# Layer 0's channel mixer by seven products of quarters, context tokens plain or as a fifth pair, and the step between the layers rebuilt

## The chip, the cores and the metric

The kernel runs on one core of one Trainium2 chip. The metric is device time in microseconds of that core for one launch, as the median of several runs. TensorE multiplies, VectorE, ScalarE and GpSimd (PE, DVE, ACT, POOL in the rows) work on tiles in SBUF, and the loads and stores spoken of here are issued from SyncE (SP).

## The reference, cut to what matters

Two layers work on 1024 latent tokens and 256 context tokens of width 1024. Each has a token mixer and then a channel mixer with 2816 hidden features; modulation vectors (six a layer, from `silu(c) @ ada_w + ada_b`) shift, scale and gate both. In the last layer the context is dropped.

```python
def _conv_ffn(h, w_gate, w_up, conv_w, conv_b, w_down):
    a = h @ w_gate
    ap = jnp.pad(a, ((0, 0), (1, 1), (0, 0)))
    a = ap[:, :-2] * conv_w[0] + ap[:, 1:-1] * conv_w[1] + ap[:, 2:] * conv_w[2] + conv_b
    return (jax.nn.silu(a) * (h @ w_up)) @ w_down
...
        x = x + g1 * _rmsnorm(y_l, norm_g[layer, 1])
        f_l = _conv_ffn(_modulate(_rmsnorm(x, norm_g[layer, 2]), sh2, sc2), ffn_w_gate[layer],
                        ffn_w_up[layer], ffn_conv_w[layer], ffn_conv_b[layer], ffn_w_down[layer])
        x = x + g2 * _rmsnorm(f_l, norm_g[layer, 3])
```

Layer 0 does the same for the context tokens (`xc`), with weights shared and a convolution of their own.

## The kernel before

**Arithmetic.** Every float32 operand is split in a high part (a cast) and a low part (the rest after it); `mm3` multiplies hi·hi, hi·lo and lo·hi, so each product of 128 contracted rows is three matmuls, up to 512 columns wide. ScalarE makes most of the high parts, GpSimd or VectorE the low ones.

**Layer 0's channel mixer (`ffn`)** walks over 22 tiles j of 128 features. For each: gate for the two latent blocks of 512 tokens (`pg`), gate and up for the 256 context tokens (`pc`), up for the latents (`pu`), each 8 contraction tiles; the convolution, Silu and product on ScalarE and VectorE; and down for the tile j-1 before, in 20 units (10 token tiles by two halves of 512 columns), each one `mm3` into a `dn` bank which VectorE adds into ten accumulators in SBUF (L909). The units are put between the groups of gate and up, as are single steps of the modulation's matmuls for later vectors (`ada_steps`, up to three a tile).

**`between_layers`** finishes the units of the last tile, does residual and norm for each token tile, transposes pairs of tiles to feature order (`to_feature`), and multiplies each block of 256 tokens by 512 columns of layer 1's input weights (480 matmuls of 256 columns, stored as `hv`); then the modulation vectors (1, 2) and (1, 3). `odd_in`, layer 1's input projection, follows.

**Layer 1's channel mixer (`ffn_seven`)** already runs by seven products: features, tokens and contraction are cut in two, four quarter blocks of each operand are combined by sums and differences, and seven products of half size replace eight (P1 to P7; `B11`, `B21`, `B22`, `T1` to `T4` on the token side, `A11`, `A12`, `A22`, `S1` to `S4` on the weight side). A pair of feature tiles is two halves (gate, up) of 7 x 12 matmuls. The hidden values' combinations go to DRAM (`gs`) and come back for the down stage (`ffn_down`, `down_operands`), again seven products, here over four pairs of token tiles; `left` loads `sr` and casts it to `sh`, `sl`, `right` does the down weights' sums.

**What sets the order.** The program is written engine-neutrally and a scheduler orders each engine's instructions; each engine then runs them strictly in that order, and a tile's next use waits until its buffers are free (`raw` has 3, `whi` and `wlo` 4 each). `ada_unit` makes one modulation vector: 8 loads of 512 KB and 32 matmuls, with the bias added as a matmul against a row of ones (L305) from `brow`; the sum is copied to `mrow`, of which there is one buffer.

Of the kernel before, what the change touches and what calls it, by code (L numbers as in the profile page):

```python
# [10 lines left out]
F32 = mybir.dt.float32  # L11
# [11 lines left out]
OUT_SLOTS = ((4, 3, 1), (3, 4, 1))  # L23
# [5 lines left out]
P = 128  # L29
# [29 lines left out]
class Kernel:  # L59
# [55 lines left out]
    def run(self):  # L115
        nc, tc = self.nc, self.tc
        with ExitStack() as es:
# [13 lines left out]
            with ExitStack() as eh:  # L131
                h = self.htiles(eh.enter_context(self.hpool()))
                self.out_proj(0, h)
                self.ffn(0, h)
                with ExitStack() as em:
                    self.odd_in(h, eh, em)
                    self.mla(em)
            with ExitStack() as es:
                self.ffn_operands(es)
                self.out_proj(1, None)  # L140
                self.ffn_seven(1, es)
# [34 lines left out]
    def differences(self, cs, names):  # L176

        F = self.F
        for n in names:
            out, x, y = {"T1": ("T1", "B12", "B11"), "T2": ("B11", "B22", "T1"), "T3": ("B12", "B22", "B12"),  # L180
                         "T4": ("B21", "B11", "B21")}[n]
            self.nc.vector.tensor_tensor(out=F[out][:, :, cs], in0=F[x][:, :, cs], in1=F[y][:, :, cs], op=ALU.subtract)

# [114 lines left out]
    def ada_unit(self, ps, tag, l, v, wp, bufs):  # L298
# [3 lines left out]
        brow = wp.tile([1, D], F32, tag="raw", name="brow", bufs=bufs)  # L302
        nc.sync.dma_start(brow, I["ada_b"][l:l + 1, v * D:(v + 1) * D])
        for g in range(4):
            nc.tensor.matmul(acc[32 * g:32 * g + 32, :256], self.ones[0:1, 0:32], brow[:, 256 * g:256 * g + 256],  # L305
                             start=True, stop=False)
        for k in range(KD):
            raw = wp.tile([P, D], F32, tag="raw", name="raw", bufs=bufs)
            nc.sync.dma_start(raw, I["ada_w"][l, k * P:(k + 1) * P, v * D:(v + 1) * D])
            for g in range(4):  # L310
                nc.tensor.matmul(acc[32 * g:32 * g + 32, :256], self.sT[:, k, :], raw[:, 256 * g:256 * g + 256],
                                 start=False, stop=k == KD - 1)
            yield
        row = self.cp.tile([P, 256], F32, tag="mrow", name="mrow", bufs=1)
        nc.vector.tensor_copy(row, acc[:, :256])
# [45 lines left out]
    def to_feature(self, ps, pool, xns, h, b0, l, which, width=512, bufs=2, every=2):  # L361
# [5 lines left out]
        for k in range(KD):  # L367
# [7 lines left out]
            eng = nc.gpsimd if k % every == 0 else nc.vector  # L375
# [6 lines left out]
    def gate_row(self, pool, l, gi, r):  # L382

        nc, I = self.nc, self.I
        ngb = pool.tile([P, D], F32, tag="xin", name="ngb", bufs=3)
        g = I["norm_g"]
        nc.sync.dma_start(ngb, bass.AP(g.tensor, (l * 4 + 1 + 2 * gi) * D, [[0, P], [1, D]]))
        gb = pool.tile([P, D], F32, name="gb", tag="gb", bufs=1)
# [4 lines left out]
    def residual(self, pool, y, gb, xsrc, xdst, pw=False):  # L393
        nc = self.nc
        x = pool.tile([P, D], F32, tag="xin", name="xin", bufs=3)
        nc.sync.dma_start(x, xsrc)
        t = pool.tile([P, D], F32, tag="yt", name="yt", bufs=2)
# [399 lines left out]
    def out_proj(self, l, h):  # L797
        nc, tc, I = self.nc, self.tc, self.I
        nt = 10 if l == 0 else 8
        with ExitStack() as es:  # L800
# [29 lines left out]
            tts = list(range(nt)) if l == 0 else [0, 1, 4, 5, 2, 3, 6, 7]  # L830
            for tt in tts:
# [9 lines left out]
                last = l == 1 and tt == tts[-1]  # L841
                if last:
                    self.wgs = self.seven_weights(self.gate_raws(0))
                    next(self.wgs)
                    wg = next(self.wgs)
                with tc.manual_schedule(engines={mybir.EngineType.PE, mybir.EngineType.DVE}) if last else ExitStack():
# [8 lines left out]
                    xns.append(self.residual(tp, y, gb, xs, xd, True))  # L855
                    if last:
                        self.first = [self.plain_products(wg, self.pse)]
                    self.flush(pst, tp, xns, h, tt, l, 3)

    def gate_raws(self, p, which="ffn_w_gate"):  # L860
        w = self.I[which][1][:, 256 * p:256 * p + 256].rearrange("(k p) c -> p k c", p=P)
        return [self.raw_w(w[:, 4 * i:4 * i + 4, :], 4, 256) for i in range(2)]

    def flush(self, ps, tp, xns, h, tt, l, which):
        if len(xns) == 2 and l == 1:
            self.to_quarters(ps, xns, (tt - 1) * P, l)
            if tt == 5:
                self.differences(slice(0, 256), ("T1", "T2", "T3", "T4"))
            xns.clear()
        elif len(xns) == 2:  # L870
            self.to_feature(ps, tp, xns, h, (tt - 1) * P, l, which, 256)
            xns.clear()


    def ffn(self, l, h):
        nc, tc, I = self.nc, self.tc, self.I
        nt = 10 if l == 0 else 8
        ctxb = l == 0
        cw = self.cw[l]
        wide = T if ctxb else NL  # L880
        with ExitStack() as eo:
            ap = eo.enter_context(tc.tile_pool(name="facc", bufs=1, reuse_waits="tile"))
            acc = [ap.tile([P, D], F32, name=f"acc{i}") for i in range(nt)]
            tp = eo.enter_context(tc.tile_pool(name="ff", bufs=2, reuse_waits="tile"))
            with ExitStack() as es:
                pgp = es.enter_context(tc.tile_pool(name="psG", bufs=1, space=PSUM, reuse_waits="tile"))
                psd = eo.enter_context(tc.tile_pool(name="psD", bufs=3, space=PSUM, side="right", reuse_waits="tile"))
                ps = es.enter_context(tc.tile_pool(name="psF", bufs=1, space=PSUM, side="right", reuse_waits="tile"))
                self.nw, self.wx = 0, tp

                def weights(j):
                    c = slice(j * P, (j + 1) * P)
                    g = self.split_w(I["ffn_w_gate"][l][:, c].rearrange("(k p) c -> p k c", p=P), KD, P)
                    u = self.split_w(I["ffn_w_up"][l][:, c].rearrange("(k p) c -> p k c", p=P), KD, P)
                    return g, u

                def down_w(j):
                    return self.split_w(I["ffn_w_down"][l, j * P:(j + 1) * P, :][:, None, :], 1, D)

                def down_units(j, g, w):  # L900
                    def unit(tt, hf):
                        o = slice(hf * 512, hf * 512 + 512)
                        c = slice(tt * P, (tt + 1) * P)
                        pd = psd.tile([P, 512], F32, tag="dn", name="dn")
                        self.mm3(pd, g[0][:, c], g[1][:, c], w[0][:, 0, o], w[1][:, 0, o], True, True)
                        if j == 0:
                            nc.scalar.copy(acc[tt][:, o], pd)
                        else:
                            nc.vector.tensor_tensor(out=acc[tt][:, o], in0=pd, in1=acc[tt][:, o], op=ALU.add)  # L909
                    return [(lambda tt=tt, hf=hf: unit(tt, hf)) for tt in range(nt) for hf in range(2)]  # L910

                def group(dst, w, b0, bn):
                    for k in range(KD):
                        self.mm3(dst, w[0][:, k, :], w[1][:, k, :], h[0][:, k, b0:b0 + bn], h[1][:, k, b0:b0 + bn],
                                 k == 0, k == KD - 1)

                def conv(j, a, src):
                    n = src.shape[1]
                    nc.scalar.activation(a, src, AF.Identity, bias=cw[:, 66 + j:67 + j], scale=cw[:, 22 + j:23 + j])
                    nc.vector.scalar_tensor_tensor(out=a[:, 1:], in0=src[:, :n - 1], scalar=cw[:, j:j + 1],  # L920
                                                   in1=a[:, 1:], op0=ALU.mult, op1=ALU.add)
                    nc.vector.scalar_tensor_tensor(out=a[:, :n - 1], in0=src[:, 1:], scalar=cw[:, 44 + j:45 + j],
                                                   in1=a[:, :n - 1], op0=ALU.mult, op1=ALU.add)
                    nc.scalar.activation(a, a, AF.Silu)

                def finish(a, src, gh, gl, eng=nc.gpsimd):
                    nc.vector.tensor_tensor(out=a, in0=src, in1=a, op=ALU.mult)
                    nc.scalar.copy(gh, a)  # L928
                    eng.tensor_tensor(out=gl, in0=a, in1=gh.bitcast(F32), op=ALU.subtract)  # L929

                steps = self.ada_steps(psd, "dn", [(0, 5), (1, 0), (1, 1)] if l == 0 else [])
                pend = []
                wgu = weights(0)
                for j in range(NF):
                    nu = len(pend)
                    done = [0]

                    def some(frac):
                        while done[0] < min(nu, math.ceil(nu * frac)):
                            pend[done[0]]()  # L940
                            done[0] += 1
                        if frac != 0.4 and frac != 0.8:
                            next(steps, None)

                    wg, wu = wgu
                    a = tp.tile([P, wide], F32, tag="a", name="a", bufs=2)
                    gh = tp.tile([P, wide], F32R, tag="gh", name="gh", bufs=2)
                    gl = tp.tile([P, wide], F32R, tag="gl", name="gl", bufs=2)
                    pg = pgp.tile([P, NL], F32, tag="pg", name="pg", bufs=1)
# [902 lines left out]
```

## Time and profile before

| | before |
|---|---|
| median of 3 runs | 3232.47 us (3231.61 to 3233.96) |
| profiled execution, its own time | 3232.91 us |
| its span | 3231.10 us |
| mean granted clock of TensorE | 0.984 |
| TensorE, VectorE, ScalarE, GpSimd busy | 95%, 54%, 36%, 28% |
| layer 0's first gate matmul; last up matmul's end | 674.29; 1599.18 us |
| end of layer 0's down; start of layer 1's projection | about 1623; 1722.33 us |
| layer 1's gate and up; its down | 2562.01 to 3001.04; to 3222 us |

The shares are means over stages with different limits, so the stretch of the change is read by its own windows and by start times on the timeline. A matmul's duration is a latency: consecutive ones overlap, and the distance between their starts is what each costs. PEclk is the granted share of the full clock of 2.4 GHz; 0.5 is the lower level, 1.2 GHz.

### The profile page before, as it was taken

The numbers are of one execution on the slowest core, as the hardware profiler recorded it, in microseconds if no ns is written. First come the engines' busy times: TensorE is split into PE (matmuls) and PEld (weight loads), VectorE is DVE, ScalarE is ACT, GpSimd is POOL, SyncE is SP. The second block draws the span as 40 slices with busy tenths as digits, with TensorE's granted clock in tenths as the row PEclk, the third lists the DMA queues.
The fourth block names the chain that finished last, engine by engine and source line by source line (L and its number), as shares of the span: only waits on it lengthen the run. The fifth ranks groups of instructions, "written<-read, shape, count | busy, mean of one in ns | idle before, by whom it ended". The sixth has DMA issues, their size and how long they took to land. (4 is left out here: it accounts for less than half of the span.)

```text
span 3231.1 us, 42059 instructions
## 1 busy us (share of the span) xinstructions
PE 3081.5 (95%) x16660; PEld 2546.0 (79%) x16660; DVE 1733.4 (54%) x2476; ACT 1175.9 (36%) x1925; POOL 905.7 (28%) x652
## 2 busy tenths in 40 slices
PE   7998899999999999999999999998999999999998
PEld 4876788777778888888777878786797788888787
DVE  5254776532434444444563434444555597788674
ACT  4212776442111111111262233333675433333343
POOL 2122223132222222222232223333321245555001
PEclk8999999999999999999999999999999999999999
DMA  7555333331221111111162451004534233333784
GB/s 235 173 172 173 83 86 120 118 118 60 66 85 60 39 40 40 40 40 40 61 227 93 137 184 31 24 29 144 175 89 138 92 96 107 98 98 107 256 287 147
DMA packets 285363, 355.72 MB, mean 110 GB/s; under 512 B 18349, under 2 KB 215522, under 8 KB 285166
## 3 DMA queue, kind: packets, MB, share of 16 engines
q1 hardware_dynamic: 253086, 310.26, 30.6%
q10 hardware_dynamic: 32080, 42.78, 3.8%
q8 instruction: 131, 2.15, 0.3%
q14 instruction: 66, 0.54, 0.0%
HBM read 271.28 MB, written 81.69 MB: 109 GB/s over the span
## 5 line engine op out<-in xcount | busy, mean ns | idle before, releaser
L909 DVE TENSOR_TENSOR acc<-dn,acc 128x512 f32<-128x512 f32 x420 | 279.7, 686 | 330.7 <-PE dn L102 330.4
L91 POOL TENSOR_TENSOR wlo<-raw,whi 128x1024 fp32r<-128x1024 f32 x94 | 225.6, 2404 | 657.8 <-ACT whi L90 627.3
L100 PE MATMUL acc<-hhi,whi 128*128 128x512 f32 (+3 forms) x632 | 236.1, 374 | 0.0
L102 PE MATMUL acc<-hhi,wlo 128*128 128x512 f32 (+3 forms) x632 | 229.9, 364 | 1.2 <-POOL wlo L91 1.2
L101 PE MATMUL acc<-hlo,whi 128*128 128x512 f32 (+3 forms) x632 | 229.5, 363 | 0.0
L90 ACT CAST whi<-raw 128x1024 fp32r<-128x1024 f32 x94 | 98.2, 1045 | 310.0 <-PE pu L101 167.0
L353 POOL TENSOR_TENSOR ss<-ss,mhalf 128x1 f32<-128x1 f32 (+1 forms) x122 | 72.0, 591 | 453.0 <-DVE ss L352 453.0
L100 PE MATMUL dn<-whi,gh 128*128 128x512 f32 x360 | 143.5, 399 | 4.3 <-DVE acc L909 4.3
L100 PE MATMUL acc<-whi,hhi 128*128 128x256 f32 (+1 forms) x464 | 143.5, 315 | 3.3 <-DVE hhi L374 3.0
L188 POOL TENSOR_TENSOR wlo<-raw,whi 128x512 fp32r<-128x512 f32 (+1 forms) x66 | 114.8, 1752 | 110.2 <-ACT whi L187 110.2
L102 PE MATMUL acc<-whi,hlo 128*128 128x256 f32 (+1 forms) x464 | 139.7, 311 | 3.8 <-POOL hlo L376 3.1
L102 PE MATMUL dn<-whi,gl 128*128 128x512 f32 x360 | 140.6, 391 | 1.2 <-POOL gl L929 1.2
L101 PE MATMUL acc<-wlo,hhi 128*128 128x256 f32 (+1 forms) x464 | 140.0, 305 | 0.8 <-POOL wlo L91 0.8
L101 PE MATMUL dn<-wlo,gh 128*128 128x512 f32 x360 | 140.6, 391 | 0.0
L100 PEld LDWEIGHTS acc<-hhi,whi 128*128 128x128 f32 (+1 forms) x632 | 118.3, 187 | 21.1 <-issue 2.1
L102 PEld LDWEIGHTS acc<-hhi,wlo 128*128 128x128 f32 (+1 forms) x632 | 118.1, 187 | 20.9 <-POOL wlo L91 1.7
L101 PEld LDWEIGHTS acc<-hlo,whi 128*128 128x128 f32 (+1 forms) x632 | 118.3, 187 | 18.3 <-issue 1.2
L188 POOL TENSOR_TENSOR wlo<-st,whi 128x1024 fp32r<-128x1024 f32 x40 | 97.3, 2435 | 101.0 <-ACT whi L187 94.4
L929 POOL TENSOR_TENSOR gl<-a,gh 128x256 fp32r<-128x256 f32 (+1 forms) x44 | 69.1, 1571 | 171.7 <-ACT gh L928 156.7
L100 PE MATMUL pg<-hhi,whi 128*128 128x512 f32 x288 | 114.1, 396 | 0.0
L101 PE MATMUL pg<-hlo,whi 128*128 128x512 f32 x288 | 112.5, 391 | 0.0
L102 PE MATMUL pg<-hhi,wlo 128*128 128x512 f32 x288 | 112.2, 390 | 0.0
(590 smaller groups left out, 8887.2 us busy)
## 6 DMA issues: line engine op xcount, KB each, us to landing
raw<-in_ada_w SPq DMA_DIRECT2D x96, 512.0 KB
raw<-in_ffn_w_down SPq DMA_DIRECT2D x69, 512.0 KB
raw<-in_ffn_w_gate SPq DMA_DIRECT2D x44, 512.0 KB
raw<-in_ffn_w_up SPq DMA_DIRECT2D x44, 512.0 KB
sr<-gs SPq DMA_DIRECT2D x12, 1408.0 KB
raw<-in_od_w_in SPq DMA_DIRECT2D x26, 512.0 KB
gs<-sx SPq DMA_DIRECT2D x11, 1024.0 KB
mx<-mix SPq DMA_DIRECT2D x18, 512.0 KB
```

The costliest lines, as they stand in the source:

```text
L90: nc.scalar.copy(hi, raw)
L91: nc.gpsimd.tensor_tensor(out=lo, in0=raw, in1=hi.bitcast(F32), op=ALU.subtract)
L100: nc.tensor.matmul(out, lh, rh, start=first, stop=False)
L101: nc.tensor.matmul(out, lh, rl, start=False, stop=False)
L102: nc.tensor.matmul(out, ll, rh, start=False, stop=last)
L188: eng.tensor_tensor(out=v(t[1]), in0=x, in1=v(t[0]).bitcast(F32), op=ALU.subtract)
L353: nc.gpsimd.tensor_tensor(out=ss, in0=ss, in1=self.mhalf[:, :ss.shape[1]], op=ALU.pow)
L909: nc.vector.tensor_tensor(out=acc[tt][:, o], in0=pd, in1=acc[tt][:, o], op=ALU.add)
L929: eng.tensor_tensor(out=gl, in0=a, in1=gh.bitcast(F32), op=ALU.subtract)
```

## The change

Layer 0's channel mixer also runs by seven products. `layer0_ffn` replaces `ffn`, with quarters of the latents (11 pairs of feature tiles, 2 halves each, 84 matmuls of 512 columns a half). The 256 context tokens are multiplied plainly within each half ("X", 48 matmuls of 256 columns, between P2 and P6). In down the two context tiles are a fifth pair beside the latents' four; the hidden values go through DRAM (`gs0`). Weights of the next half are prepared while a half runs; the low parts of the four plain weight quarters are VectorE's, those of the sums GpSimd's. Differences of the token quarters are made in place as the output projection finishes its pairs, whose order for layer 0 is now that of layer 1. The first pair's gate runs product by product as its operands come. Modulation steps go one to a half, behind P1.

`layer0_last` does residual and norm, for the tiles 4 to 7 and 9 and then 0 to 3 and 8, as the last product finishes them. The step between the layers takes blocks of two tiles in the order 512, 768, 0, 256, 1024, with three modulation steps each; the low parts there are all VectorE's. `ada_unit` adds the bias on VectorE from four broadcast loads into `mrow`.

```diff
@@ ada_unit @@
-        brow = wp.tile([1, D], F32, tag="raw", name="brow", bufs=bufs)
-        nc.sync.dma_start(brow, I["ada_b"][l:l + 1, v * D:(v + 1) * D])
+        row = self.cp.tile([P, 256], F32, tag="mrow", name="mrow", bufs=1)
         for g in range(4):
-            nc.tensor.matmul(acc[32 * g:32 * g + 32, :256], self.ones[0:1, 0:32], brow[:, 256 * g:256 * g + 256],
-                             start=True, stop=False)
+            nc.sync.dma_start(row[32 * g:32 * g + 32, :],
+                              bass.AP(I["ada_b"].tensor, (l * 6 + v) * D + 256 * g, [[0, 32], [1, 256]]))
...
-        nc.vector.tensor_copy(row, acc[:, :256])
+        nc.vector.tensor_tensor(out=row, in0=acc[:, :256], in1=row, op=ALU.add)
@@ out_proj @@
-            tts = list(range(nt)) if l == 0 else [0, 1, 4, 5, 2, 3, 6, 7]
+            tts = [0, 1, 4, 5, 2, 3, 6, 7, 8, 9][:nt]
...
+                        if l == 0 and tt > 3:
+                            self.differences_in_place(cs)
@@ layer0_ffn @@
+                    def weights(which, p, r=None):
...
+                        put([(A11, first), (A12, second)], ("A11", "A12"), nc.vector)
+                        put([(A21, first), (A22, second)], ("A21", "A22"), nc.vector)
+                        for o, x, y, op in ((self.s1, A21, A22, ALU.add), (A21, A11, A21, ALU.subtract),
+                                            (A11, self.s1, A11, ALU.subtract), (A12, A12, A11, ALU.subtract)):
+                            nc.vector.tensor_tensor(out=o, in0=x, in1=y, op=op)
+                        put([(r0, lambda t: t)], ("S2", "S3"), nc.gpsimd)
+                        put([(self.s1, first), (A12, second)], ("S1", "S4"), nc.gpsimd)
...
+                    alone("P1", "pp", "A11", "B11")
+                    alone("P2", "pp", "A12", "B21")
+                    part("T2", F["B11"], every)
+                    alone("P6", "pp", "S2", "T2")
+                    part("T3", F["B12"], every)
+                    alone("P7", "pp", "S3", "T3")
+                    for k, t in enumerate(t1):
+                        nc.vector.tensor_tensor(out=t, in0=F["B22"][:, k, :], in1=F["B11"][:, k, :], op=ALU.subtract)
+                        part("T1", t, k)
+                    alone("P5", "ada", "S1", "T1")
+                    part("B22", F["B22"], every)
+                    alone("P3", "Y", "S4", "B22")
...
+                    context()
+                    alone("P4", "X", "A22", "T4")
+                    x = context_products(wg)
...
+                        for n, a, b in (("P1", "A11", "B11"), ("P2", "A12", "B21"), ("X", 0, 0), ("P6", "S2", "T2"),
+                                        ("P7", "S3", "T3"), ("P5", "S1", "T1"), ("P3", "S4", "B22"), ("P4", "A22", "T4")):
...
+                for b0 in (512, 768, 0, 256, 1024):
+                    self.to_feature([psx], tb, C[tt:tt + 2], h, b0, 1, 0, 256, 2, None)
+                    for _ in range(3):
+                        next(steps, None)
...
@@ ffn_down @@
-        nq = 4
+        nq = len(accs)
+        t1s, t2s = ([0, 1, 2, 3], [4, 5, 6, 7]) if l else ([0, 1, 2, 3, 8], [4, 5, 6, 7, 9])
...
-                    if n < 6:
+                    if n < 6 and (l or q < 2):
                         down.right(n + 1, 2 * q, 2 * q + 2)
...
+                if n < 6 and not l:
+                    down.right(n + 1, 4, 6)
```

VectorE between the last context tile's residual (`yt`, `xin`) and the first products, before; `hhi`, `hlo` are the tokens' parts:

```order
L400 TENSOR_TENSOR yt<-yt,xin 128x1024
L352 TENSOR_SCALAR ss<-ss 128x1
L402 TENSOR_SCALAR xin<-yt,ss 128x1024
L374 CAST hhi_5610<-hf 128x256 x2
L376 TENSOR_TENSOR hlo_5613<-hf,hhi_5610 128x256
```

and now, where X, ada and Y are PSUM banks that hold T1, and FB the quarters:

```order
L404 TENSOR_TENSOR yt<-yt,xin 128x1024
L1011 TENSOR_TENSOR X<-FB_5617,FB_5618 128x512 x2
L1011 TENSOR_TENSOR ada<-FB_5617,FB_5618 128x512
L356 TENSOR_SCALAR ss<-ss 128x1
L1011 TENSOR_TENSOR Y<-FB_5617,FB_5618 128x512
L406 TENSOR_SCALAR xin<-yt,ss 128x1024
L937 TENSOR_TENSOR s_5604<-raw 128x512
L914 TENSOR_TENSOR T2l<-FB_5618,T2h 128x2048
L914 TENSOR_TENSOR T3l<-FB_5619,T3h 128x2048
```

The low parts of T2 and T3 stand behind the residual and the T1 differences.

ScalarE at the end of layer 0's gate and up, before (`gh` is a hidden tile, `acc` the down sum):

```order
L928 CAST gh<-a 128x1024
L90 CAST whi<-raw 128x1024
L1341 ACTIVATE gh,ss<-acc_6679 128x1024
L1347 ACTIVATE a,ss<-gh 128x1024
L1341 ACTIVATE gl,ss<-acc_6680 128x1024
```

and now, at the change from P1 to P5 in layer 0's down (`X` are weight sums, `C` the output quarters):

```order
L1441 CAST B11h<-X_11357 128x1024
L1441 CAST B11l<-X_11358 128x1024
L1441 CAST B21h<-X_11359 128x1024
L1441 CAST Hch<-X_11361 128x1024
L1504 COPY C_11371<-pp 128x512
L1504 COPY C_11372<-pp 128x512
L1504 COPY C_11373<-Y 128x512
L1504 COPY C_11374<-pp 128x512
L1504 COPY C_11379<-pp 128x512
L1441 CAST Hcl<-X_11362 128x512
L1441 CAST B21l<-X_11360 128x1024
L1475 CAST sh<-sr 128x1408 x6
```

P5's first left operand, `sh`, is cast behind six casts of weight sums and the five copies of P1's results.

SyncE at the program's start, the second unit's loads, before:

```order
L309 DMA raw<-in_ada_w 128x1024
L285 DMA cr_229<-in_ffn_conv_b 22x128
L303 DMA brow<-in_ada_b 1x1024
L309 DMA raw<-in_ada_w 128x1024 x8
L74 DMA raw<-in_ev_w_in 128x4x256 x2
```

and now:

```order
L314 DMA raw<-in_ada_w 128x1024
L291 DMA cr_228<-in_ffn_conv_b 22x128
L310 DMA mrow<-in_ada_b 32x256 x4
L314 DMA raw<-in_ada_w 128x1024 x8
L75 DMA raw<-in_ev_w_in 128x4x256 x2
```

The four bias loads go into the tile that the first unit's transposes read, and the eight weight loads are queued behind them.

## Rows read from the trace of the kernel before

**Rows 1.** Page, part 1: busy time, share of the span, instructions of each engine.

```profile
PE 3081.5 (95%) x16660; PEld 2546.0 (79%) x16660; DVE 1733.4 (54%) x2476; ACT 1175.9 (36%) x1925; POOL 905.7 (28%) x652
```

**Rows 2.** Windows, one stretch a row: us, busy of each engine, PEclk, DMA share, GB/s.

```profile
754.00:1550.00 796.00, 795.97 (x4003) 659.04 (x4003) 332.32 (x492) 149.21 (x173) 195.19 (x95) 1.00 0.17 51
1599.00:1623.00 24.00, 18.48 (x76) 13.10 (x74) 20.34 (x32) 8.90 (x12) 9.27 (x7) 1.00 0.49 174
2567.00:2576.00 9.00, 4.47 (x18) 2.33 (x17) 3.86 (x4) 5.24 (x10) 3.45 (x3) 0.67 0.24 91
2612.00:2982.00 370.00, 370.00 (x1598) 298.99 (x1598) 298.74 (x332) 125.22 (x154) 195.22 (x97) 1.00 0.33 106
```

**Rows 3.** Timeline of PE, up and context products: start, us, instruction, wait before.

```profile
1299.45 0.39 PE L100 MATMUL pu<-hhi,whi 128*128 128x512 f32 x1
1299.68 0.39 PE L101 MATMUL pu<-hlo,whi 128*128 128x512 f32 x1
...
1332.11 0.28 PE L102 MATMUL pc<-hhi,wlo 128*128 128x256 f32 x1
1332.23 0.28 PE L100 MATMUL pc<-hhi,whi 128*128 128x256 f32 x1
```

**Rows 4.** Timeline of PE: a modulation step between matmuls; two half starts, layer 1.

```profile
696.61 0.28 PE L102 MATMUL pc<-hhi,wlo 128*128 128x256 f32 x1
696.82 0.64 PE L311 MATMUL ada<-raw,sT 128*32 128x256 f32 x8
697.38 0.50 PE L100 MATMUL pu<-hhi,whi 128*128 128x512 f32 x1
...
2962.12 0.39 PE L100 MATMUL pp<-B11h,whi 128*128 128x512 f32 x1
...
2981.58 0.39 PE L100 MATMUL pp<-B11h,whi 128*128 128x512 f32 x1
```

**Rows 5.** Timeline of PE: the boundaries from layer 0's gate to layer 1's projection.

```profile
674.29 0.48 PE L100 MATMUL pg<-hhi,whi 128*128 128x512 f32 x1
...
1599.18 0.39 PE L100 MATMUL dn<-whi,gh 128*128 128x512 f32 x1
...
1622.80 0.39 PE L102 MATMUL dn<-whi,gl 128*128 128x512 f32 x1
...
1714.03 1.50 PE L311 MATMUL ada<-raw,sT 128*32 128x256 f32 x24
...
1722.33 1.22 PE L100 MATMUL acc<-whi,hhi 128*128 128x512 f32 x2 [0.18 <-ACT whi L90]
...
1743.14 0.60 PE L1411 MATMUL ct<-ident,cf 128*128 128x128 f32 x4
```

**Rows 6.** Groups by form: operation, shapes, count | busy us, mean ns | idle before.

```profile
L1133 DVE TENSOR_TENSOR u<-u,pp 128x512 f32<-128x512 f32 x77 | 51.2, 680 | 0.8 <-PE pp L102 0.5
L1079 DVE TENSOR_TENSOR a<-a,u 128x512 f32<-128x512 f32 x44 | 48.1, 1096 | 1.2
...
L188 POOL TENSOR_TENSOR wlo<-st,whi 128x1024 fp32r<-128x1024 f32 x40 | 97.3, 2435 | 101.0 <-ACT whi L187 94.4 <-DVE a L1079 6.6
```

**Rows 7.** Timelines of SP, PE and ACT at layer 1's change from P1 to P5.

```profile
3024.33 0.37 SPq L1240 DMA_DIRECT2D sr<-gs  x1
...
3031.60 0.39 PE L102 MATMUL pp<-te,B22l 128*128 128x512 f32 x1
3033.99 0.62 PE L100 MATMUL pp<-whi,sh 128*128 128x512 f32 x1 [1.99 <-ACT sh L1244]
3034.40 0.63 PE L101 MATMUL pp<-wlo,sh 128*128 128x512 f32 x1
...
3032.57 2.63 ACT L1244 CAST sh<-sr 128x1408 fp32r<-128x1408 f32 x2
```

**Rows 8.** Timeline of SP and PE at the program's start.

```profile
21.17 11.11 SPq L309 DMA_DIRECT2D raw<-in_ada_w  x8
25.15 0.69 PE L322 MATMUL adat<-ident,mrow 128*128 128x128 f32 x2 [0.55 <-DVE mrow L315]
```

More of the change, by code (lines that the diff above doesn't have):

```diff
@@ L1 @@
+import itertools
 import math
@@ L22 @@
 MLA_EARLY = 2
-OUT_SLOTS = ((4, 3, 1), (3, 4, 1))
+OUT_SLOTS = ((4, 4, 0), (3, 4, 1))
 IN_ORDER = "a3b2!!c1!!d0L"
@@ L182, in differences, with differences_in_place @@
             self.nc.vector.tensor_tensor(out=F[out][:, :, cs], in0=F[x][:, :, cs], in1=F[y][:, :, cs], op=ALU.subtract)
+    def differences_in_place(self, cs):
+        F = self.F
+        for out, x, y, op in (("B12", "B22", "B12", ALU.subtract), ("B11", "B12", "B11", ALU.add),
+                              ("B21", "B21", "B11", ALU.subtract)):
+            self.nc.vector.tensor_tensor(out=F[out][:, :, cs], in0=F[x][:, :, cs], in1=F[y][:, :, cs], op=op)
     def parts(self, t, r, eng):
@@ L311, in ada_unit @@
                 nc.tensor.matmul(acc[32 * g:32 * g + 32, :256], self.sT[:, k, :], raw[:, 256 * g:256 * g + 256],
-                                 start=False, stop=k == KD - 1)
+                                 start=k == 0, stop=k == KD - 1)
             yield
-        row = self.cp.tile([P, 256], F32, tag="mrow", name="mrow", bufs=1)
-        nc.vector.tensor_copy(row, acc[:, :256])
+        nc.vector.tensor_tensor(out=row, in0=acc[:, :256], in1=row, op=ALU.add)
         if v in (2, 5):
@@ L864, in flush @@
[L864 to L907, printed above, removed]
-                        else:
[L909 to L949, printed above, removed]
-                    pu = ps.tile([P, NL], F32, tag="pu", name="pu", bufs=1)
-                    group(pg[:, :512], wg, 0, 512)
-                    some(0.2)
-                    group(pg[:, 512:], wg, 512, 512)
-                    conv(j, a[:, :NL], pg)
-                    some(0.4)
-                    if ctxb:
-                        pc = ps.tile([P, 2, 256], F32, tag="pc", name="pc", bufs=1)
-                        group(pc[:, 0, :], wg, NL, 256)
-                        group(pc[:, 1, :], wu, NL, 256)
-                        conv(j, a[:, NL:], pc[:, 0, :])
-                        finish(a[:, NL:], pc[:, 1, :], gh[:, NL:], gl[:, NL:])
-                    some(0.6)
-                    wd = down_w(j)
-                    group(pu[:, :512], wu, 0, 512)
-                    some(0.8)
-                    if j + 1 < NF:
-                        wgu = weights(j + 1)
-                    group(pu[:, 512:], wu, 512, 512)
-                    finish(a[:, :NL], pu, gh[:, :NL], gl[:, :NL])
-                    some(1.0)
-                    pend = down_units(j, (gh, gl), wd)
@@ L972, in ffn, with layer0_last, last @@
                 for _ in steps:
                     pass
-                self.wx = None
-            if l == 0:
-                self.between_layers(h, acc, tp, pend, psd)
+            return h
+    def layer0_last(self, pool, C, order):
+        nc = self.nc
+        gb = [self.gate_row(pool, 0, 1, r, f"gb{r}", 2) for r in range(2)]
+        def last(tt):
+            rows = slice(tt * P, (tt + 1) * P)
+            x = pool.tile([P, D], F32, tag="xin", name="xin", bufs=2)
+            nc.sync.dma_start(x, self.x1[rows, :])
+            t = C[tt]
+            rs = self.rstd_of(pool, t, "y", pool.tile([P, D], F32, tag="junk", name="junk", bufs=1), True)
+            nc.vector.scalar_tensor_tensor(out=t, in0=t, scalar=rs, in1=gb[tt // 8], op0=ALU.mult, op1=ALU.mult)
+            nc.vector.tensor_tensor(out=t, in0=t, in1=x, op=ALU.add)
+            nc.sync.dma_start(self.x2[rows, :], t)
+            rs = self.rstd_of(pool, t, "x", x, True)
+            nc.vector.tensor_scalar(out=t, in0=t, scalar1=rs, scalar2=None, op0=ALU.mult)
+        return last
@@ L1014, in all_weights @@
             def all_weights(which, p):
-                for w in self.seven_weights(self.gate_raws(p, which), tp):
+                for w in self.seven_weights(self.gate_raws(l, p, which), tp):
                     pass
@@ L1136, with down_operands @@
             ("P2", 1, "B21"))
-    def down_operands(self, l, gs):
+    def down_operands(self, l, gs, rest=None, raws=("T2", "T3"), parts=("T1", "B22")):
         nc, k = self.nc, self
@@ L1188, in open @@
                 self.X = X
+                if pool is None:
+                    self.sets.append([self.pair() for _ in range(4)] + self.sets[0][4:])
+                    return
                 tile_ = lambda i, n: [pool.tile([P, n, 512], F32R, name=f"t{i}{b}") for b in "hl"]
@@ L1218, in right, with ffn_down @@
                         self.T[n][p] = hi[:, i], lo[:, i]
-        return Down()
-    def ffn_down(self, l, gs, bank, down, accs):
+        return Down(rest, raws, parts)
+    def ffn_down(self, l, gs, bank, down, accs, ctiles=None, then=None):
         nc, tc = self.nc, self.tc
         NP = NF // 2
-        nq = 4
+        nq = len(accs)
+        t1s, t2s = ([0, 1, 2, 3], [4, 5, 6, 7]) if l else ([0, 1, 2, 3, 8], [4, 5, 6, 7, 9])
         with ExitStack() as es:
-            sp = es.enter_context(tc.tile_pool(name="dS", bufs=2, side="right", reuse_waits="tile"))
-            cp = es.enter_context(tc.tile_pool(name="dC", bufs=1, side="right", reuse_waits="tile"))
-            tp = es.enter_context(tc.tile_pool(name="dT", bufs=1, reuse_waits="tile"))
+            right = lambda name, bufs=1: es.enter_context(tc.tile_pool(name=name, bufs=bufs, side="right", reuse_waits="tile"))
+            if l:
+                sp, cp = right("dS", 2), right("dC")
+                tp = es.enter_context(tc.tile_pool(name="dT", bufs=1, reuse_waits="tile"))
+            else:
+                sp, cp, tp = right("dS", 2), ctiles, None
             ex = ExitStack()
@@ L1248, in ffn_down @@
             last = None
-            lefts = [(n, q) for n in range(7) for q in range(nq)][4:]
-            ready = [None] * 4
+            lefts = [(n, q) for n in range(7) for q in range(nq)][nq:]
+            ready = [None] * nq
             for n, (name, _, b) in enumerate(self.DOWN):
@@ L1254, in ffn_down @@
                     fp = es.enter_context(tc.tile_pool(name="fin", bufs=3, side="right", reuse_waits="tile"))
-                    last = self.ffn_last(fp, C, (4, 5, 6, 7, 0, 1, 2, 3))
-                    for q in range(nq):
-                        last(q + nq)
+                    last = (self.ffn_last if l else self.layer0_last)(fp, C, t2s + t1s)
+                    for tt in t2s:
+                        last(tt)
                 for q in range(nq):
-                    if lefts and (n, q) > (0, 2):
+                    if lefts and (n, q) > (0, nq - 2):
                         ready.append(left(*lefts.pop(0)))
-                    if n < 6:
+                    if n < 6 and (l or q < 2):
                         down.right(n + 1, 2 * q, 2 * q + 2)
@@ L1286, in ffn_down @@
                         add(c11, c11)
-                        last(q)
+                        last(t1s[q])
+                        if q == 1 and then:
+                            then()
+                if n < 6 and not l:
+                    down.right(n + 1, 4, 6)
+            return C
     def ffn_last(self, pool, acc, order):
```

359 lines of the change are left out of this document (280 added, 79 removed).

## Prediction, written before the changed kernel ran

> **What bounds the kernel now.** I read the page's shares first: TensorE is busy 95% of the span, the next engine, VectorE, 54% [rows 1]. That is an average, so I read the windows next. Through layer 0's gate, up and down (754 to 1550 us) TensorE is busy 795.97 of 796.00 us while VectorE works 332 us; through layer 1's gate and up, which run by seven products of quarters already, it is busy 370.00 of 370.00, with VectorE at 298.74 of 370 (81%) [rows 2]. So both stages are bound by the number of matmuls, and layer 1 shows what the new form costs in steady state, on this chip, in this program. Where TensorE does wait is at seams: 18.48 of 24 us at the end of layer 0's down, and 4.47 of 9 us with the clock at 0.67 where layer 1 makes its first operands [rows 2]. The prediction is therefore a count of matmuls by a spacing, and then the seams one by one.
>
> **The prices.** Durations of matmuls in the groups are latencies that overlap; the price is the distance from start to start. It is 0.23 us for a 512-column matmul (1299.45 to 1299.68) and 0.12 us for a 256-column one [rows 3]; over a whole seven-product half it is sharper: from 2962.12 to 2981.58 there are 84 matmuls in 19.46 us, 0.2267 us each if the boundary takes 0.42 [rows 4].
>
> The Trainium skill (TensorE: Matmul & The Clock Gate, section "Back-to-back issue gap") gives 512/2.4 + 2.5, or 215.8 ns, for such a matmul in isolation. The rows are 5% above it; by the page's figure the removed matmuls below would be worth 92.6 us and not 97.3. The measured spacing decides.
>
> **What goes.** Layer 0's gate and up are 22 tiles x 2 weights x 2 blocks x 8 x 3 = 2112 wide matmuls for the latents and 22 x 2 x 8 x 3 = 1056 narrow ones for the context. Seven products of quarters make the 2112 into 22 halves x 84 = 1848; the narrow ones stay ("X"). Down is 22 x 20 x 3 = 1320 and becomes 7/8 of it, 1155, since context tokens are a fifth pair. That is 429 matmuls, 429 x 0.2267 = **97.3 us** less on an engine that is otherwise full. The rest decides whether it arrives. I sum the stretch from the first gate matmul (674.29) to the third tile of layer 1's input projection (1743.14), 1068.9 us before [rows 5].
>
> **Sum of the stretch after.**
> Start of the stage. After the last y of the output projection TensorE has P1 and P2 (24 matmuls, 5.4 us) ready, then needs T2 and T3: 2048-element splits which VectorE does behind the residual of the last context tile and four T1 subtractions (the order shows it), then 16 transposes of the context tiles. The nearest row is layer 1's own start, which lost 4.5 us at a 0.67 clock in a window of 9 [rows 2]; there tokens came in two halves, here all parts come behind one chain. I take 14 us, the transposes included, from 5 to 22.
> Gate and up: 22 halves of 19.46 [rows 4] and 48 x 0.12 = 5.76 [rows 3] are 25.2, in all 554.9. VectorE: 15.7 us a half in layer 1 (81% of 19.46 [rows 2]); four of the weights' low parts move from GpSimd to it, 4 x 1 us by the nearest two-SBUF-input row (1096 ns beside GpSimd's work, 680 without [rows 6]); the context's convolution and product add 1.5. That is 21 of 25.2 us, 84%, against the 81% at which TensorE did not wait. GpSimd is relieved. So I price waits in steady state at nothing; if that cover is gone it is rival C.
> Modulation steps: one insertion of eight records lengthened 0.12 to 0.77 us (696.61 to 697.38), 0.65 more [rows 4]. Twenty are in the halves and four behind them, 24 x 0.65 = 15.6. Before, the same 24 were cut in two pieces each: 924.9 us from 674.29 to 1599.18 [rows 5], less 22 x 27.5 + 21 x 13.6 = 891, leaves 34 us for them and the start.
> Down: 1155 x 0.2267 = 261.8. At layer 1's seam P1 to P5 the first matmul came 2.39 us after the last (3031.60, 3033.99), then 0.41 apart at half clock; ScalarE's cast of sh started at 3032.57, 8.2 us after the load's issue at 3024.33 [rows 7]. After, on ScalarE six casts and five copies of C stand ahead of that cast, and the load stands in SyncE's queue behind weight loads that wait for VectorE. Ends 6 and 20; I take 12, nearer to the row. Five later seams with more pairs each: 4. Together 277.8.
> The turn to layer 1's input. The old down tail took 23.6 us from 1599.18 to 1622.80 for 60 matmuls worth 13.6 [rows 5]; it is in the 1068.9 and goes. Then 480 narrow matmuls (57.6), 80 transposes (8), sixteen modulation steps (10.4), and a start behind the last residual chain on VectorE: 6 of waiting, 2 of half clock. That is 84. Before: 91.2 (1622.80 to 1714.03) and then 8.3 until 1722.33 for modulation steps that waited on their loads [rows 5]; after, those stand between the token blocks.
> Two tiles of the projection: 72 x 0.2267 = 16.3, and 6 because their weights' slots come free only when the last token block ends; low parts on GpSimd take 2.4 us each [rows 6]. Before 20.8 (1722.33 to 1743.14) [rows 5].
> 14 + 554.9 + 15.6 + 277.8 + 84 + 22.3 = 968.6, so **100 us** less.
>
> **Outside the stretch.** At the program's start the second unit's eight weight loads were issued from 21.17; the bias row now goes into the one mrow tile, so its DMAs stand on SyncE until the first unit's transposes are read (25.15 [rows 8], about 26 with the read), and eight loads wait behind them: +4 (1 to 6), since the first transposes of the input wait for that unit. The bias matmuls that go give back about 1 in layer 1. The new order of the output projection changes no count for layer 1. Net: 100 - 4 + 1 = 97. The profiled execution took 3232.91, with a span of 3231.10; the median of three runs is 3232.47. 3232.9 - 97 = **3136**.
>
> **Rivals.** A, the forecast: matmul-bound halves, seams as priced. B, seams cost double (start 22, P1 to P5 20, the turn and the latents 8 more, later seams 4 more): +28, 3164. For it: layer 1's own operands stalled, and the orders on VectorE and ScalarE are strict. Against: each has matmuls ready in part. B', all seams at their low ends: 3136 - 9 - 6 - 5 - 3 = 3113. C, VectorE's strict order: with 84% load one late accumulation holds back a product bank and TensorE waits 2 us in each of 22 halves, +44: 3180. For it: two-input operations already stretch from 680 to 1096 ns [rows 6]. Against: 81% with no wait at all over 370 us [rows 2]. D, on the other side: GpSimd stops VectorE outright. Nine two-input operations a half, each stopped on average for half of a 2.4 us GpSimd operation [rows 6], add 10.8 to 21 us, 31.8 against 25.2: 6.6 x 22 = +145, 3281, slower. It decides from 29.6 us of VectorE per half, where the 97 are eaten up. Against: in layer 1 such operations took 0.4 us longer and not 1.2.
>
> The Trainium skill (SBUF — State Buffer, section "Who interferes with whom") is the rule behind D: a VectorE instruction with two SBUF inputs contends with a GpSimd instruction that reads SBUF, and whichever starts second is held until the first ends. The 1096 against 680 ns agree that they contend and show a mean cost far below a whole GpSimd operation.
>
> E, that the quarters do not stand for what they say: too few matmuls would go only if the context stayed inside the down's plain form, which the five pairs exclude; time within 0.2% of before needs seams of 90 us more.
>
> **How the numbers follow.** A 0.66, B 0.12, B' 0.06, C 0.11, D 0.03, between C and no change 0.02. A alone reaches from 3118 to 3158. The range takes in B and most of B' and leaves C and D out: 3114 to 3168. Faster by over 0.2% (6.5 us, about what a measurement of this kernel can tell from no change): 0.95; within it 0.02; slower 0.03.
>
> **What would show it.** The changed profile should have TensorE dense, at 25.2 us a half with no wait line in the middle of gate and up; some 12 us of waits for T2, T3 and T4 after the last y; a wait for sh of about 10 us at P1 to P5; a short wait for hhi before the first token block; no 4 us wait on a modulation load between the layers; and the first input transposes about 4 us later. A half of 27 us or more, with waits on VectorE, is C; TensorE busy less than eight tenths in the halves is D. I am wrong if the seams together exceed 60 us or stay under 15.

## The result, and the profile after

The changed kernel is slower by 1.5%: 3281.89 us median (3279.05 to 3285.26, 4 runs) against 3232.31, a ratio of 1.0153 with a 95% interval of 1.0135 to 1.0171. The forecast was 3136, in a range of 3114 to 3168, with a chance of 0.03 for slower. The profiled execution took 3285.26 us with a span of 3283.5.

First the page, busy time of each engine and its clock row, where [rows 1] had TensorE at 3081.5 us and 95%:

```profile
span 3283.5 us, 41673 instructions
...
PE 3023.4 (92%) x16135; PEld 2503.0 (76%) x16135; DVE 1942.6 (59%) x2671; ACT 1262.4 (38%) x2056; POOL 792.9 (24%) x568
...
PEclk7999999989999999999999999999999999999999
```

TensorE has less to do, as forecast, and yet the span grew by 52 us: it waits more. The lists of TensorE's waits over the whole span say for what (waited for, total, times, longest); the first line is of the kernel before, the others of the changed one:

```profile
PE ada L311 <- DMA raw<-in_ada_w: 14.8, 14, 4.4
...
PE ada L316 <- DMA raw<-in_ada_w: 107.7, 39, 10.0
...
PE X L101 <- ACT sh L1475: 12.3, 1, 12.3
...
PE pp L101 <- ACT T2h L913: 6.5, 1, 6.5
```

The modulation steps wait for their weight loads, 108 us in all and 14.8 before, 75.1 of them in 19 waits of 3.5 to 4.3 us in the halves of gate and up. A window through those halves, to be held against [rows 2] (us, busy PE, PEld, DVE, ACT, POOL, PEclk, DMA share, GB/s):

```profile
800.00:1200.00 400.00, 352.79 (x1774) 291.49 (x1773) 241.47 (x325) 101.77 (x150) 81.50 (x37) 0.93 0.26 83
```

TensorE is busy 88%, its clock is granted at 0.93, and no other engine is near its limit: VectorE 60%. Two halves, by the first matmul of P1 (timeline of TensorE):

```profile
977.53 0.39 PE L101 MATMUL pp<-B11h,whi 128*128 128x512 f32 x1
...
1008.80 0.39 PE L101 MATMUL pp<-B11h,whi 128*128 128x512 f32 x1
...
1040.50 0.39 PE L101 MATMUL pp<-B11h,whi 128*128 128x512 f32 x1
```

The nineteen halves with a step from 753.75 to 1359.88 take 31.90 us each on average, where 25.9 was forecast.

**How one half waits.** The engines around the start at 1008.80, in timelines of ScalarE, GpSimd, SyncE and TensorE (start, length, instruction, idle before and what ended it):

```profile
1006.00 1.05 ACT L927 CAST whi<-raw 128x1024 fp32r<-128x1024 f32 x1 [4.45 <-PE pp L102]
1008.76 0.62 ACT L927 CAST whi<-s 128x512 fp32r<-128x512 f32 x1 [1.71 <-PE pp L102]
1009.29 0.61 ACT L927 CAST whi<-raw 128x512 fp32r<-128x512 f32 x1
...
1007.13 2.73 POOL L928 TENSOR_TENSOR wlo<-raw,whi 128x1024 fp32r<-128x1024 f32 x1 [24.41 <-ACT whi L927]
1009.83 1.88 POOL L928 TENSOR_TENSOR wlo<-s,whi 128x512 fp32r<-128x512 f32 x1
1011.67 1.87 POOL L928 TENSOR_TENSOR wlo<-raw,whi 128x512 fp32r<-128x512 f32 x1
...
1013.57 0.33 SPq L314 DMA_DIRECT2D raw<-in_ada_w  x1
...
1018.29 1.08 PE L316 MATMUL ada<-raw,sT 128*32 128x256 f32 x8 [4.33 <-DMA raw<-in_ada_w]
1019.30 0.80 PE L102 MATMUL Y<-B21l,whi 128*128 128x512 f32 x1
1019.90 0.63 PE L103 MATMUL Y<-B21h,wlo 128*128 128x512 f32 x1
```

Read in order of time it is a chain. When TensorE's P3 has read the slot of `whi` that the weight sums S2 and S3 of the next half take, ScalarE casts them (1006.00, released by PE). Behind that cast GpSimd makes three low parts without a pause (1007.13 to 1013.54); the last of them gives back a `raw` buffer. The sums S1 and S4 wait for another slot, which P4 gives back at 1008.76, but their first cast is done at 1009.38, before GpSimd is free at 1009.86, so P4 holds nothing up. This is so in every half: in the nineteen from 753.75 to 1359.88 GpSimd waits 20 times before these low parts, once in each and once at the edge, and not between the three. In the buffer given back the step's load starts at 1013.57, and it is there 4.7 us later. TensorE has meanwhile done P4, P1 and ten matmuls of P2, and stands from 1013.97 to 1018.29. The chain starts at TensorE's own P3, so no lead can build up: every half pays. After the wait matmuls come 0.60 apart at first and not 0.23; the windows show the clock at its lower level, 0.50, and then rising (columns as above):

```profile
1018.29:1020.33 2.04, 2.04 (x11) 1.03 (x12) 0.00 (x0) 0.00 (x0) 0.00 (x0) 0.50 1.03 413
1020.33:1022.00 1.67, 1.67 (x12) 1.67 (x11) 0.00 (x0) 0.00 (x0) 0.00 (x0) 0.72 1.02 395
```

### The profile page after: what moved, and what is told of

The parts are those of the page before. It is cut to its first block, busy times and chain, and to the rows that moved or that the text cites. A ratio compares the mean times of both kernels' runs of the same rounds, so it can differ in the third digit from the quotient of the medians.

```text
span 3283.5 us, 41673 instructions
## 1 busy us (share of the span) xinstructions
PE 3023.4 (92%) x16135; PEld 2503.0 (76%) x16135; DVE 1942.6 (59%) x2671; ACT 1262.4 (38%) x2056; POOL 792.9 (24%) x568
## 5 line engine op out<-in xcount | busy, mean ns | idle before, releaser
L928 POOL TENSOR_TENSOR wlo<-raw,whi 128x1024 fp32r<-128x1024 f32 (+1 forms) x44 | 101.8, 2313 | 543.6 <-ACT whi L927 543.6
L927 ACT CAST whi<-raw 128x512 fp32r<-128x512 f32 x132 | 86.9, 689 | 351.2 <-PE X L102 174.6
L92 POOL TENSOR_TENSOR wlo<-raw,whi 128x1024 fp32r<-128x1024 f32 (+1 forms) x41 | 98.4, 2404 | 325.7 <-ACT whi L91 302.1
L316 PE MATMUL ada<-raw,sT 128*32 128x256 f32 x768 | 74.8, 470 | 108.1 <-DMA raw<-in_ada_w 107.7
L928 DVE TENSOR_TENSOR wlo<-raw,whi 128x512 fp32r<-128x512 f32 x88 | 56.9, 687 | 152.1 <-ACT whi L927 152.0
L1475 ACT CAST sh<-sr 128x1408 fp32r<-128x1408 f32 x54 | 73.9, 1372 | 170.4 <-PE pp L102 105.0
L316 PEld LDWEIGHTS ada<-raw,sT 128*32 128x32 f32 x768 | 19.5, 119 | 139.1 <-DMA raw<-in_ada_w 103.0
L101 PE MATMUL X<-Hch,whi 128*128 128x256 f32 x352 | 111.4, 316 | 0.0
L102 PE MATMUL X<-Hcl,whi 128*128 128x256 f32 x352 | 110.2, 313 | 0.0
L103 PE MATMUL X<-Hch,wlo 128*128 128x256 f32 x352 | 109.1, 310 | 0.0
```

Source lines behind the costliest of these rows:

```text
L92: nc.gpsimd.tensor_tensor(out=lo, in0=raw, in1=hi.bitcast(F32), op=ALU.subtract)
L101: nc.tensor.matmul(out, lh, rh, start=first, stop=False)
L102: nc.tensor.matmul(out, lh, rl, start=False, stop=False)
L103: nc.tensor.matmul(out, ll, rh, start=False, stop=last)
L927: nc.scalar.copy(v(t[0]), x)
L928: eng.tensor_tensor(out=v(t[1]), in0=x, in1=v(t[0]).bitcast(F32), op=ALU.subtract)
```

## The experiments

**e1: the step before the weights.** Three `raw` buffers serve two weight loads and one step load a half. Each request takes the buffer that was given back longest ago: in the changed kernel the first weight load leaves when a step's matmuls end (987.09, on SyncE's timeline), the second behind GpSimd's low part of S2 and S3 (1009.89), and the step's, asked for last, behind GpSimd's last (1013.57).

```diff
-                                    wu = weights("ffn_w_up", p)
                                     next(steps, None)
+                                    wu = weights("ffn_w_up", p)
...
-                                wg = weights("ffn_w_gate", p + 1)
                                 next(steps, None)
+                                wg = weights("ffn_w_gate", p + 1)
```

> Edit: in both places of layer 0's halves the modulation step is taken before the next weights are prepared and not after, so that its load takes the raw buffer that the previous step's matmuls gave back, and the weights' second load takes the one that GpSimd gives back last. Theory T1 (the step's load starts only when GpSimd's last low part has given its buffer back, lands 4.6 us later, and TensorE stands before the step for 4 us, after which it runs at half clock for a while): the halves fall from 31.95 us to between 25.9 and 26.5, no wait on in_ada_w in the halves, 3282 - 20 x 5.5 to 6 = 3162 to 3172 us. Rival T2 (the ring of weight loads, casts and low parts sets the period, and the step only shows it): halves stay at 30 us or more, the wait moves to the first weights' casts or low parts, 3250 to 3290 us. Rival T3 (VectorE's load, the prediction's C and D): halves stay at 30 us with waits on VectorE.

Measured: 3171.0 us (3166.78 to 3174.09, 4 runs), a ratio of 0.9807 to the kernel before (0.9791 to 0.9824). On the timelines of SyncE and TensorE the load is issued at 989.67 in the half before, and the step at 1012.81 no longer waits:

```profile
989.67 0.45 SPq L314 DMA_DIRECT2D raw<-in_ada_w  x1
...
983.96 0.39 PE L101 MATMUL pp<-B11h,whi 128*128 128x512 f32 x1
...
1009.98 0.39 PE L101 MATMUL pp<-B11h,whi 128*128 128x512 f32 x1
...
1012.81 0.64 PE L316 MATMUL ada<-raw,sT 128*32 128x256 f32 x8
```

The half takes 26.02 us. T1 stands, T2 and T3 fall: with the same loads, casts, low parts and VectorE work, TensorE is busy in every microsecond of the window shown; through all the halves with a step it waits once, 2.1 us until 1146.48, for VectorE's `mod`:

```profile
800.00:1130.00 330.00, 330.00 (x1786) 273.72 (x1785) 246.16 (x325) 102.64 (x153) 86.12 (x39) 1.00 0.33 111
```

**e6: the step later.** The buffers are asked for as in the changed kernel, but TensorE comes to the step behind P7, some 12 us later than before. The two `next(steps, None)` move from the branch of P1 to that of P7:

```diff
                                 if n == "P1":
                                     wu = weights("ffn_w_up", p)
-                                    next(steps, None)
...
+                                elif n == "P7":
+                                    next(steps, None)
```

> Edit: the weights still ask for their buffers before the modulation step, as in the changed kernel, but the step is taken behind P7 of the half and not behind P1, so that TensorE comes to it some 10 us later while GpSimd gives the buffer back at the same time. T1 (lateness of the load against the step's place): the wait of 4 us goes, halves of 25.9 to 26.5, 3162 to 3175 us. If instead the buffer order itself holds up the ring (the next weights' first load now waits for the step's matmuls): halves of 28 or more with waits for casts or low parts.

Measured: 3168.43 us in one run; halves of 25.99 us (983.01 to 1009.00) without any wait. From 725 to 1280 there is one, of 2.3 us, at 1273.42 in down. So it is neither the order of the buffers nor the load as such, but that the load starts too late for where the step stands.

**e7: GpSimd's last low parts on VectorE.** The other end of the chain:

```diff
-                        put([(self.s1, first), (A12, second)], ("S1", "S4"), nc.gpsimd)
+                        put([(self.s1, first), (A12, second)], ("S1", "S4"), nc.vector)
```

> Edit: the changed kernel with the low parts of S1 and S4, the last to read a raw buffer, on VectorE in place of GpSimd; the step's place and buffer are as in the changed kernel. T1: the buffer comes free about 2 to 3 us earlier, so the wait before the step falls from 4 to between 1 and 2.5 us and the halves to 28 to 30.5, 3210 to 3255 us. The prediction's C and D (VectorE's load): VectorE goes from some 70% to 75% of the half, halves get longer than 31.95 us, and the time is above 3282.

Measured: 3215.52 us in one run. The wait before the step falls to 2.0 us (39.7 us in 20 waits), the halves to 28.0 ((1009.63 - 953.56) / 2). The chain is shorter: in the half from 1009.63 the load leaves after 3.1 us (1012.69), in the like half of the changed kernel after 5.2 (977.53, 982.75). VectorE, which by the rivals C and D was the danger, got more work, and the kernel gained 66 us. Against C that speaks; against D it doesn't by itself, since GpSimd, which D has in VectorE's way, lost two of its three low parts:

```profile
800.00:1200.00 400.00, 372.43 (x1963) 309.50 (x1962) 269.85 (x388) 114.65 (x168) 35.28 (x14) 0.98 0.31 97
```

**e2: no step in the halves.** Both `next(steps, None)` are deleted; the 24 steps run where the list is emptied, at the start of down.

> Edit: no modulation steps in the halves; all 24 come behind them, where the kernel already empties the list at the start of the down stage. T1: every half is 25.2 to 26.3 us, 20 x 6 = 120 us less there; the 24 steps then cost the time of their loads beside the down weights' loads, 30 to 60 us, so 3190 to 3225 us. T2: halves stay at 30 us or more even without any step, and the time is 3290 us or above.

Measured: 3175.05 us in one run. A half without a step (timeline of TensorE) and the window:

```profile
1001.61 0.39 PE L101 MATMUL pp<-B11h,whi 128*128 128x512 f32 x1
...
1026.83 0.39 PE L101 MATMUL Y<-B11h,whi 128*128 128x512 f32 x1
...
800.00:1200.00 400.00, 400.00 (x2099) 340.89 (x2098) 301.50 (x405) 128.92 (x191) 104.39 (x48) 1.00 0.27 89
```

The half takes 25.22 us, the figure of the prediction's sum, and VectorE is busy 75% while TensorE is full. The time came out below its range: the steps in down cost less than was thought, though the wait before P5 rose to 19.0 us. With e1, a step that has its data costs 0.80 us (0.65 was priced). Of the 31.90 us, then, 25.22 are products, 0.80 the step, 3.95 the wait (75.1 / 19), and 1.9 is left for the lower clock behind it; in the half shown above the clock alone makes 1.5 (half of 2.04 us, and 0.28 of 1.67).

**e3 and e8: the seam from P1 to P5.** e3 asks for P5's first two left operands before P1's weights are made; e8 also issues the first load of `sr` from GpSimd. The condition that asks for the later ones changes with it and is not shown.

```diff
             ready = [None] * nq
+            if not l:
+                ready += [left(*lefts.pop(0)) for _ in range(2)]
...
+                    eng = nc.gpsimd if not l and (i, q) == (3, 0) else nc.sync
+                    eng.dma_start(self.sraw[:, :, :n], gs[i, :, :, q * P:q * P + n].rearrange("p f t -> f p t"))
```

> Edit: in layer 0's down the first two left operands of P5 are asked for before P1's weights are prepared, so that the load of sr stands ahead of the waiting weight loads on SyncE; ScalarE's order stays. If SyncE's queue holds the load back (issued 1432.70, cast at 1442.67 after 4.42 us of waiting for it): the wait before P5 falls from 12.3 to about 8 us, 3277 to 3279. If ScalarE's casts and copies alone set it: no change, 3282.

> Edit: as e3_sr_early, and the first load of sr is issued from GpSimd, which has nothing queued there, not from SyncE. If SyncE's queue is what holds the load: the load lands before ScalarE is through with its casts and copies, sh is cast from about 1438 and not 1442.67, the wait falls from 12.3 to 7 or 8 us, 3275 to 3278. If the buffer or the data hold it: no change, 3278 to 3282.

Measured: 3277.76 and 3279.28 us, one run each, too near to 3281.89 for a verdict on the time. The waits tell more. In the changed kernel P5's first matmul came at 1444.08, 12.70 us after P1's last (1431.38). In e3 the load still stood behind the weight loads (issued 1430.62) and the wait was 11.2 where about 8 was expected; one kernel's two profiles differ by as much here (10.6 and 11.5 in e5_all and again), so e3's gain is not clear of that. In e8 (POOL, ACT, PE rows):

```profile
1401.49 1.25 POOL L1472 DMA_DIRECT2D sr<-gs  x1 [35.30 <-DMA raw<-in_ffn_w_down]
...
1436.57 2.67 ACT L1476 CAST sh<-sr 128x1408 fp32r<-128x1408 f32 x2
...
1438.02 0.79 PE L101 MATMUL X<-whi,sh 128*128 128x512 f32 x1 [8.47 <-ACT sh L1476]
```

The load left 29 us earlier than in e3 and the wait fell to 8.5; e9_best has 8.6. So SyncE's queue made 3 to 4 us of the 12. Of the rest ScalarE's casts and copies ahead of `sh`, without a pause from 1430.81 to 1436.57, are the most.

**e4: the bias loads last.** In `ada_unit` the four loads into `mrow` move behind the eighth weight load:

```diff
+            if k == KD - 1:
+                for g in range(4):
+                    nc.sync.dma_start(row[32 * g:32 * g + 32, :],
+                                      bass.AP(I["ada_b"].tensor, (l * 6 + v) * D + 256 * g, [[0, 32], [1, 256]]))
```

> Edit: the bias loads of a modulation vector are issued behind its eighth weight load and not ahead of the first. If the mrow buffer holds the second vector's loads back at the program's start: the first input transposes go from 47.56 back to about 42 us. Whether the end follows: by the prediction 4 to 6 us less, 3276; but the first gate matmul came only 0.7 us later than before though the start was 6 us later, so by the rival (hidden behind later waits) 0 to 2 us less.

Measured: 3281.64 us in one run. The first input transposes came at 40.13 and not 47.56, so `mrow` did hold the loads; the first gate matmul came 3.4 us earlier (671.53 and not 674.97). Of 7.4 us at the start 3.4 were left there. That moment varies: in the seven profiles with the early bias loads (the changed kernel, e1 to e3, e6 to e8) it lies from 672.86 to 677.20, in the four with late ones (e4, e5_all twice, e9) from 671.53 to 672.43, 3.5 us apart in the mean. The time, one run against a median of four, doesn't show them.

**e5 and e9: together.** e5_all is e1, e3 and e4; e9_best is e1, e4 and e8.

> Edits of e1, e3 and e4 together (step first, sr early, bias loads late). Sum of what each gave alone against 3282: 111 + 4 + 0 to 1 = 3166 us; if the start's 4 us arrive (first gate matmul 3.4 us earlier in e4's profile), 3163; if the seams overlap, 3168 to 3171, no better than e1 alone.

> Edits of e1, e4 and e8 together: step first, bias loads late, first load of sr from GpSimd. In e5_all the wait before P5 was 10.6 us; with the load landed early it should be 8 to 9, so 1 to 3 us less than e5_all beside it: 3160 to 3164 us. If the seams hide one another: no difference from e5_all.

> The same kernel as e5_all, on the same chip as e9_best for the comparison: 3163 to 3168 us.

Measured: e5_all 3165.44 us (0.9786, 0.9766 to 0.9806), and again 3164.95 (0.978, 0.9766 to 0.9794) beside e9_best with 3162.21 (0.978, 0.9767 to 0.9793). These last two beat the kernel before by over 2%; the intervals of the first e5_all and of e1 end just short of that. Between e9_best and e5_all no difference can be told, and e1 alone has most of the gain.

## Why the prediction was wrong, point by point

**The step that failed** is "Modulation steps": "one insertion of eight records lengthened 0.12 to 0.77 us, 0.65 more [rows 4]. Twenty are in the halves". The price of the matmuls was right, 0.80 measured in e1. What was not asked is whether their data would be there. In the row it was taken from, the kernel before had the load in time; the change put the step's load third in line for three buffers, so that it got the one that GpSimd frees last. It cost 6.7 us a half (31.90 - 25.22) and not 0.65, 121 us more over twenty. With it falls "I price waits in steady state at nothing": the cover was looked for on VectorE alone.

**D's number, not D's reason.** The rival D gave 3281. It gave it by VectorE at 31.8 us a half; VectorE was busy 60% of the time, and in e1, with GpSimd and VectorE doing the same work, TensorE is full. That the times agree is chance. VectorE's load was over-estimated too: 75% in e2, not 84%. Two of its operations with both inputs in SBUF, in e2 and then in e7, with GpSimd at 26% and at 9% of the window (groups by form):

```profile
L1085 DVE TENSOR_TENSOR a<-u,a 128x512 f32<-128x512 f32 x30 | 23.8, 792 | 0.8
...
L1138 DVE TENSOR_TENSOR u<-u,a 128x640 f32<-128x640 f32 x8 | 14.4, 1798 | 0.3
...
L1085 DVE TENSOR_TENSOR a<-u,a 128x512 f32<-128x512 f32 x28 | 19.3, 688 | 0.5
...
L1140 DVE TENSOR_TENSOR u<-u,a 128x640 f32<-128x640 f32 x7 | 5.8, 824 | 0.2
```

That is the rule weighed in the prediction (the Trainium skill, SBUF — State Buffer, section "Who interferes with whom"), and the trace agrees that the two contend: 0.1 us in the mean for the first, 1.0 us for the second, which in e2 runs while GpSimd is at work (1003.40, GpSimd from 999.94 to 1006.36). An estimate of what it costs in all: VectorE is busy 38.17 us in two halves of e2 (951.16 to 1001.61), and 38.43 in two of e7 (953.56 to 1009.63), of which four low parts of 0.685 are the additional ones. That leaves 1.2 us a half, where D took 10.8. The 680 ns that the prediction calls "without" is of an operation with one input in PSUM; the 688 of e7 bears the figure out.

**What held.** 429 matmuls fewer (TensorE's records fell by 525, from 16660 to 16135, and 96 of them are the bias matmuls), each half 25.2 us (25.22 in e2), TensorE bound by its matmuls once the step had its data, the seam P1 to P5 at 12 us (12.70 from matmul to matmul), some 12 us of waits at the start of the stage (12.3), two tiles of the projection at 22.3 (22.7, from 1773.24 to 1795.96).

**Terms that were too small.** From the first gate matmul to the third tile of the projection the changed kernel took 1121.0 us (674.97 to 1795.96) and not 968.6; the steps are 121 of the 152. With the steps set right e1, at 3171, is still 35 us over the forecast. The start of the stage cost 22.4 us and not 14: in e2 the first two halves took 72.8 us (676.60 to 749.40) against 50.4. Its rows in the changed kernel:

```profile
687.14 0.80 PE L101 MATMUL pp<-T2h,whi 128*128 128x512 f32 x1 [6.53 <-ACT T2h L913]
...
688.94 0.80 PE L101 MATMUL pp<-T3h,whi 128*128 128x512 f32 x1 [1.01 <-ACT T3h L913]
...
690.59 0.80 PE L102 MATMUL pp<-T2l,whi 128*128 128x512 f32 x1 [0.85 <-DVE T2l L914]
```

The waits are as described, but they are followed by matmuls at the lower clock (granted 0.50 from 687.14 to 691.00, 0.67 in the mean from 687.14 to 697.00), for which the term has no figure of its own. Down with its four steps took 293 us and not 280 (1385.19 to 1678.50): its first pair of tiles took 15.2 us (1386.19 to 1401.40), with a 3.0 us wait of a step for its load, and each of the next three 7.6. The turn took 94.7 and not 84 (1678.50 to 1773.24), with 5.6 and 3.2 us of waiting and a granted clock of 0.73 in the mean up to 1697.00:

```profile
1686.12 1.15 PE L374 MATMUL tr<-ident,C 128*128 128x128 f32 x4 [5.61 <-ACT hf L376]
...
1693.64 0.56 PE L101 MATMUL acc<-whi,hhi 128*128 128x256 f32 x1 [3.24 <-DVE hhi L378]
```

At the program's start the price was 4 us and the transposes came 6 later, but at the first gate matmul 0.7 was left, which is less than that moment varies between profiles. In e1 the three terms are over by 8.5, 9.3 (289.7 from 1273.43 to 1563.16) and 10.8 us (94.8 to 1657.92), 29 of the 35; the rest is not divided further. So the sign that the prediction gives for being wrong, seams over 60 us, is met apart from the steps. By the forecast's own prices for what is counted, the start, down, the turn and the two tiles held 22.4, 28.9, 18.7 and 6.4 us of seams, 76 and not 44 (14, 16, 8 and 6). That is near the sum of rival B (28 more), though not seam by seam: the start came at B's 22, P1 to P5 stayed at 12 where B has 20.

## What to carry to other kernels

When a small step is put into a loop that is otherwise dense, ask when its load may start, not only what its instructions cost: follow its buffer back to the last reader, on whichever engine that is, and add the load's time. If that chain begins at the loop's own matmuls, every turn pays and no slack elsewhere helps. Where streams of different urgency share a few rotating buffers, the order in which they ask decides who gets the late one; the exchange of two lines, in two places, was worth 111 us here.

## What was not expected of the hardware

A wait of 3.95 us on TensorE, in the mean, made a half 5.9 us longer (31.90 less 25.22 and 0.80 for the step): the clock was granted at 0.50 behind it, and the matmuls came up to 0.60 apart (1019.30 to 1019.90) before they were back at 0.23. And an engine at 75%, in strict order beside GpSimd, cost TensorE nothing: in e2's window VectorE was busy 301.50 of 400 us and TensorE all 400.
